# Full 128-token sample tile in the retention, smaller first loads, ones on TensorE at both ends, and the first head's values in a misc PSUM buffer

## The chip, the cores and the metric

The kernel runs on one core of one Trainium2 chip. The metric is the device time of one execution in microseconds (us). The version before takes a median of 1504.3 us over three runs (1504.21 to 1505.61).

## The reference

One step of a hybrid decoder layer over N = 320 tokens: a prompt of 256 and 8 samples of 8 tokens. One input projection feeds two groups of heads: 64 S5 groups (a complex diagonal scan, GELU, a sigmoid GLU) and 8 retention heads. Then an output projection, a SwiGLU feed-forward part and a last RMSNorm.

```python
h = rms_norm(x, norm_mix)
proj = h @ w_in
u, q, k, v, g = jnp.split(proj, [...], axis=-1)
s5_out, s5_re, s5_im = s5_mixer(u, ...)
...
# retention, per head, per chunk of tokens
scores = jnp.einsum('bhnd,bhmd->bhnm', qc, kc) * mask
o = jnp.einsum('bhnm,bhme->bhne', scores, vc) + jnp.einsum('bhnd,bhde->bhne', qc, r) * q_decay
r_new = r * chunk_decay + jnp.einsum('bhmd,bhme->bhde', kc * k_decay, vc)
...
o = (o - mu) * lax.rsqrt(var + NORM_EPS)          # per head
ret_out = jax.nn.silu(g) * o * ret_gn_w
x = x + jnp.concatenate([s5_out, ret_out], axis=-1) @ w_out
h2 = rms_norm(x, norm_ffn)
x = x + (jax.nn.silu(h2 @ w_gate) * (h2 @ w_up)) @ w_ffn_out
y = rms_norm(x, norm_final)
```

D_MODEL is 2048, the head dimension 128, D_FF 5632; all is float32.

## The kernel before

All activations lie transposed: features on the 128 partitions, the 320 tokens along the free axis (0 to 255 the prompt, 256 to 319 the samples). A float32 product is made of three fast ones: each operand is split into `hi` (rounded) and `lo` (the rest), and `gemm` (L122) issues hi·hi, hi·lo and lo·hi for each 128-row tile of the contraction. A weight tile of 512 KB goes through `wload` (L108): SP's DMA to `raw`, ScalarE casts `hi`, VectorE subtracts `lo`. Such a chain runs for each of the 420 weight loads, and TensorE consumes them one after another.

TensorE's order is written by the program itself (`manual_schedule`, L780): instructions stand in the order in which Python issues them. The small work of the retention heads and of the S5 chunks is written as generators. Each yields a delay from the table `DL` (L774), and between two k-tiles of a GEMM `run_due` (L86) runs those that are due by a made-up clock, `clk.now`, which every matmul advances by a cost that the call gives: 0.4 a k-tile in `gemm`, 0.12 a transpose in `tr`, the first argument of `mm`. So a changed cost, or a matmul more or less, can shift where later small work lands between the k-tiles. Orders on VectorE and ScalarE come from a scheduler with priorities (`tc.high_priority`).

PSUM: two accumulators `acc` for GEMMs (L125); two `misc` buffers (L222) that transposes, scores (`pss`), state products (`psr`, `psu`) and the S5's `pk_` and `pt` share; `po` one; `pb` and `py` one each for S5.

The front (L784 to L826) computes the first two S5 inputs from raw x while x streams in: four chunks c of 640 KB of x with two weight pieces of 256 KB each, split by `split_x` (L248). Chunk 0's x comes in two halves. GEMMs go to `py0` and `pb0`. Then come the RMSNorm's sums (`rstd_bcast`, L181, whose reciprocal root `rsqrt`, L170, works on integers and three Newton steps), then q, k, v (`ps_p`) of head 0, each rotated by `rot` (L594). Heads follow: `do_q`, `do_k`, `do_v`, `do_g`, and S5's input `do_u`.

A head, in `head_k` (L609) and `head_v` (L631): transposes of k (`pst`) and v (`pst2`) in pieces of 128, 128 and 64 tokens; `kd`, the decayed k; `pss`, scores; `sm`, `smp`, masked scores; `po`, outputs, in which the samples' part is `smp` times vT plus eight small products of `qg` with the samples' state `rt`; `psr`, the prompt's new state; `pn`, outputs transposed back; then `update` (L698): `psu`, two products of `kd` and `vb`, which VectorE adds to `rt`.

S5's chunk: `bst` and `kst` give `pb` (L531), VectorE multiplies it by `tab` (`t`), forms `ends` and `w`, scans (L551), multiplies again (`v`); ScalarE and VectorE do the GELU of the chunk before (`y`, `u`).

The tail (L1061): last sums of squares (`ps_r`, `ps_l`), reciprocal root on VectorE, `ps_r2` broadcasts it by six passes, and x1 is scaled and stored.

## Time and profile before

| what | us |
|---|---|
| median of three runs | 1504.3 |
| the profiled execution | 1504.93 |
| its span | 1503.0 |
| TensorE busy | 1471.0 |
| VectorE busy | 865.7 |
| ScalarE busy | 607.5 |
| mean granted TensorE clock | 0.992 |

The page's second part cuts the span into 40 slices of 37.6 us and gives the busy tenths of each engine:

```profile
PE   8989999999999999999999999999999999999996
DVE  8987767877655674444444444445444444444454
ACT  5545444544434553333333333333333333333352
PEclk9999999999999999999999999999999999999998
```

The first slice and the last are those with idle TensorE; VectorE is fullest in the first eight slices or so, the heads' part. In the chain of waits:

```profile
PE 68%; DVE 0%; ACT 0%; issue 0%; DVEq 0%
```

The chain that ended last runs along TensorE. In the rows of a timeline the first number is the start in us from the span's start, the second the duration, then engine, line, operation, output and inputs, and in brackets how long the engine was idle before it and what released it.

### The profile page before, as it was taken

The page shows a single profiled execution, that of the slowest core. Times are in us where ns is not written, and L with a number is a line of the kernel's source. Part 1 is how long each engine was busy: PE and PEld are TensorE (multiplying, and loading weights), DVE is VectorE, ACT ScalarE, POOL GpSimd, SP SyncE. Part 2 cuts the span into 40 slices and gives each one's busy share as a digit, 9 for nine tenths or more (in the row PEclk, how much of TensorE's full clock was granted, in tenths as well). Part 3 has the DMA queues.
Part 4 walks back from the last instruction along what each step waited for, and adds up shares of the span by engine and source line. Part 5 has one row for each costly group of instructions (what it writes and reads, how often), then busy time and mean ns, then how long its engine had stood idle before and what let it go on. Part 6 is the DMA issues. An engine that isn't in the chain of part 4 may idle for free.

```text
span 1503.0 us, 26157 instructions
## 1 busy us (share of the span) xinstructions
PE 1471.0 (98%) x10554; PEld 1441.3 (96%) x10554; DVE 865.7 (58%) x1502; ACT 607.5 (40%) x967; POOL 79.6 (5%) x167
## 2 busy tenths in 40 slices
PE   8989999999999999999999999999999999999996
PEld 7989999898999999999999999999999999999996
DVE  8987767877655674444444444445444444444454
ACT  5545444544434553333333333333333333333352
POOL 1331310300000000000000000000000000000001
PEclk9999999999999999999999999999999999999998
DMA  8343444342464444444444445544444544434442
GB/s 284 127 153 119 140 138 147 125 144 94 143 228 142 153 144 166 149 146 155 150 146 154 130 144 158 167 147 153 145 126 151 181 144 153 151 124 150 149 146 108
DMA packets 77335, 224.49 MB, mean 149 GB/s; under 512 B 14752, under 2 KB 26400, under 8 KB 77216
## 3 DMA queue, kind: packets, MB, share of 16 engines
q1 hardware_dynamic: 77216, 222.83, 45.3%
q8 instruction: 83, 1.36, 0.4%
q14 instruction: 36, 0.29, 0.1%
HBM read 213.84 MB, written 7.63 MB: 147 GB/s over the span
## 4 chain that ended last, share of the span: by engine, by line
PE 68%; DVE 0%; ACT 0%; issue 0%; DVEq 0%
PE ps_fg L128 7%; PE ps_fo L128 7%; PE ps_fo L130 7%; PE ps_fu L128 7%; PE ps_fg L130 7%; PE ps_fu L130 7%; PE ps_fu L129 7%; PE ps_fg L129 7%; PE ps_fo L129 7%; PE ps_o L129 1%; PE ps_o L128 1%; PE ps_o L130 1%; PE ps_g L129 1%; PE ps_g L130 1%; PE ps_g L128 1%; DVE x L163 0%
## 5 line engine op out<-in xcount | busy, mean ns | idle before, releaser
L118 DVE TENSOR_TENSOR lo<-raw,hi 128x1024 fp32r<-128x1024 f32 (+1 forms) x420 | 471.4, 1123 | 410.9 <-ACT hi L117 410.6
L117 ACT CAST hi<-raw 128x1024 fp32r<-128x1024 f32 (+1 forms) x420 | 406.4, 968 | 732.4 <-PE ps_fo L129 189.3
L128 PE MATMUL ps_fo<-ahi,hi 128*128 128x320 f32 x704 | 217.5, 309 | 0.0
L129 PE MATMUL ps_fo<-alo,hi 128*128 128x320 f32 x704 | 217.5, 309 | 0.0
L128 PE MATMUL ps_fg<-hhi,hi 128*128 128x320 f32 x704 | 217.5, 309 | 0.0
L130 PE MATMUL ps_fo<-ahi,lo 128*128 128x320 f32 x704 | 217.5, 309 | 0.0
L129 PE MATMUL ps_fg<-hlo,hi 128*128 128x320 f32 x704 | 217.4, 309 | 0.0
L129 PE MATMUL ps_fu<-hlo,hi 128*128 128x320 f32 x704 | 217.4, 309 | 0.0
L128 PE MATMUL ps_fu<-hhi,hi 128*128 128x320 f32 x704 | 217.4, 309 | 0.0
L130 PE MATMUL ps_fg<-hhi,lo 128*128 128x320 f32 x704 | 217.4, 309 | 0.0
L130 PE MATMUL ps_fu<-hhi,lo 128*128 128x320 f32 x704 | 217.4, 309 | 0.0
L128 PE MATMUL ps_p<-xhi,hi 128*128 128x320 f32 x592 | 191.1, 323 | 1.4 <-ACT v__757 L751 1.4
L130 PE MATMUL ps_p<-xhi,lo 128*128 128x320 f32 x592 | 184.4, 311 | 0.0
L129 PE MATMUL ps_p<-xlo,hi 128*128 128x320 f32 x592 | 184.3, 311 | 0.0
L129 PEld LDWEIGHTS ps_fg<-hlo,hi 128*128 128x128 f32 x704 | 132.4, 188 | 0.0
L128 PEld LDWEIGHTS ps_fo<-ahi,hi 128*128 128x128 f32 x704 | 132.4, 188 | 0.0
L128 PEld LDWEIGHTS ps_fu<-hhi,hi 128*128 128x128 f32 x704 | 132.4, 188 | 0.0
L129 PEld LDWEIGHTS ps_fu<-hlo,hi 128*128 128x128 f32 x704 | 132.4, 188 | 0.0
L130 PEld LDWEIGHTS ps_fo<-ahi,lo 128*128 128x128 f32 x704 | 132.4, 188 | 0.0
L128 PEld LDWEIGHTS ps_fg<-hhi,hi 128*128 128x128 f32 x704 | 132.4, 188 | 0.0
L130 PEld LDWEIGHTS ps_fu<-hhi,lo 128*128 128x128 f32 x704 | 132.4, 188 | 0.0
L130 PEld LDWEIGHTS ps_fg<-hhi,lo 128*128 128x128 f32 x704 | 132.3, 188 | 0.0
(402 smaller groups left out, 1978.6 us busy)
## 6 DMA issues: line engine op xcount, KB each, us to landing
raw<-w_fi SPq DMA_DIRECT2D x176, 512.0 KB, 3.6
raw<-w_in SPq DMA_DIRECT2D x76, 512.0 KB, 3.9
raw<-w_fo SPq DMA_DIRECT2D x64, 512.0 KB, 3.5
raw<-w_out SPq DMA_DIRECT2D x32, 512.0 KB, 3.6
raw<-w_fo SPq DMA_DIRECT2D x64, 192.0 KB, 2.4
rt<-r SPq DMA_DIRECT2D x8, 512.0 KB, 4.0
rs_o<-rt SPq DMA_DIRECT2D x8, 512.0 KB, 3.3
raw<-w_glu SPq DMA_DIRECT2D x8, 512.0 KB, 3.6
```

The lines of the kernel that those rows point to most:

```text
L117: act.copy(hi[:, :m], raw[:, :m])
L118: dve.tensor_tensor(lo[:, :m], raw[:, :m], f(hi[:, :m]), SUB)
L128: pe.matmul(ps, hi, xhi[:, k], start=k == 0, stop=False)
L129: pe.matmul(ps, hi, xlo[:, k], start=False, stop=False)
L130: pe.matmul(ps, lo, xhi[:, k], start=False, stop=k == nk - 1)
```

## The change

The edits, by place:

- **Retention's sample tile.** Transposes of k and v now take tokens 192 to 319, so the samples sit in partitions 64 to 127 of a full tile; `smp`, `bmk`, `vb` and the masks move there (mask rows of prompt tokens are zero). The samples' `po` products with `smp` are issued ahead of the eight `qg` products. The cost of one `pss` product rises from 0.11 to 0.22.
- **`rsqrt`**: the shift and the multiply become one operation.
- **Front**: `vec` is loaded by ScalarE's queue; x and the first weights come in pieces of k-tiles (0,2), (2,4), (4,8) and so on, with x's first two tiles one by one; `split_x` puts three of the first four xhi on ScalarE; TensorE's blocks follow the pieces.
- **`keep_warm`**: matmuls on ones into an unread accumulator: 8 ahead of the first GEMM, 3 and 9 in the last norm.
- **Head 0's v** accumulates in a misc buffer (`ps_pv`); `finish_norm` copies `rtok` once.

```diff
         clk.now += 0.12
+    onesr = ones.bitcast(F32R)
+    def keep_warm(n):
+        pt = ps_acc.tile([P, 512], F32, name="warm_ps", tag="acc", bufs=2)
+        for _ in range(n):
+            pe.matmul(pt, onesr, onesr.unsqueeze(1).to_broadcast([P, 4, P]), start=True, stop=True)
...
     def rsqrt(t, y, tmp):
-        ts(tmp.bitcast(I32), t.bitcast(I32), 1, ALU.logical_shift_right)
-        ts(y.bitcast(I32), tmp.bitcast(I32), -1, MUL, 0x9EF759DF, ADD)
+        ts(y.bitcast(I32), t.bitcast(I32), -0.5, MUL, float(0x1EF759DF), ADD)
...
         ps = sums(acc, "ps_r")
+        if last is not None:
+            keep_warm(3)
...
                 stt(ms, sums(last(), "ps_l"), -0.5 / D, ms, MUL, ADD)
+            if last is not None:
+                keep_warm(9)
...
     kdc = mp.tile([P, H, 3], F32, name="kdc")
-    bmk = mp.tile([64, 4], F32, name="bmk")
+    bmk = mp.tile([P, 4], F32, name="bmk")
...
         pool.memset(qgs[i], 0.0)
-    smp = mp.tile([64, NB, 32], F32, name="smp")
+    smp = mp.tile([P, NB, 32], F32, name="smp")
...
             k = 4 * c + i
-            if c == 0 or c == 3 and i % 2:
+            if k == 0 or c == 3 and i % 2:
...
     def head_k(h, q_, qg, k_, R):
...
         pst = misc("pst")
-        for i in range(3):
-            m = P if i < 2 else 64
-            tr(pst[:m, P * i:P * i + P], k_[:, P * i:P * i + m])
+        for i, s in enumerate(STARTS):
+            tr(pst[:, P * i:P * i + P], k_[:, s:s + P])
...
         for i in range(3):
-            m = P if i < 2 else 64
-            act.mul(kd[:m, i], pst[:m, P * i:P * i + P], kdc[:m, h, i:i + 1])
+            act.mul(kd[:, i], pst[:, P * i:P * i + P], kdc[:, h, i:i + 1])
...
         mm(0.22, pss[:, 256:384], k_[:, P:256], q_[:, P:256], start=True, stop=True)
-        mm(0.11, pss[0:64, 384:448], k_[:, 256:320], q_[:, 256:320], start=True, stop=True)
+        mm(0.22, pss[:, 384:448], k_[:, 192:320], q_[:, 256:320], start=True, stop=True)
...
         tt(sm[:, 256:384], pss[:, 256:384], mk[:, 0:P], MUL)
-        tt(smp[:, :, 0:NS], pss[0:64, 384:448].rearrange("p (b t) -> p b t", t=NS),
-           mk[0:64, NP:320].rearrange("p (b t) -> p b t", t=NS), MUL)
+        tt(smp[64:128, :, 0:NS], pss[64:128, 384:448].rearrange("p (b t) -> p b t", t=NS),
+           mk[64:128, NP:320].rearrange("p (b t) -> p b t", t=NS), MUL)
...
     def head_v(h, v_, qg, rt, R):
...
         pst2 = misc("pst2")
-        for i in range(3):
-            m = P if i < 2 else 64
-            tr(pst2[:m, P * i:P * i + P], v_[:, P * i:P * i + m])
+        for i, s in enumerate(STARTS):
+            tr(pst2[:, P * i:P * i + P], v_[:, s:s + P])
...
         for i in range(3):
-            m = P if i < 2 else 64
-            act.mul(vT[:m, i], pst2[:m, P * i:P * i + P], rtok[:m, i:i + 1])
-        vb = mp.tile([64, 4, P], F32, name="vb", tag="vb", bufs=1)
-        pool.tensor_tensor(vb, vT[0:64, 2].unsqueeze(1).to_broadcast([64, 4, P]),
-                           bmk.unsqueeze(2).to_broadcast([64, 4, P]), MUL)
+            act.mul(vT[:, i], pst2[:, P * i:P * i + P], rtok[:, i:i + 1])
+        vb = mp.tile([P, 4, P], F32, name="vb", tag="vb", bufs=1)
+        pool.tensor_tensor(vb[64:128], vT[64:128, 2].unsqueeze(1).to_broadcast([64, 4, P]),
+                           bmk[64:128].unsqueeze(2).to_broadcast([64, 4, P]), MUL)
...
         mm(0.22, po[:, 1], sm[:, 256:384], vT[:, 1], start=False, stop=True)
+        for g in range(2):
+            mm(0.22, po[:, 2 + g], smp[:, 4 * g:4 * g + 4].rearrange("p b t -> p (b t)"), vT[:, 2],
+               start=g == 0, stop=False, skip_group_check=True)
...
             for j in range(4):
-                mm(0.06, po[32 * j:32 * j + 32, 2 + g], qg[:, 4 * g + j], rt[:, 4 * g + j], start=True,
-                   stop=False, tile_position=(0, 32 * j))
-            mm(0.22, po[:, 2 + g], smp[:, 4 * g:4 * g + 4].rearrange("p b t -> p (b t)"), vT[0:64, 2],
-               start=False, stop=True)
+                mm(0.06, po[32 * j:32 * j + 32, 2 + g], qg[:, 4 * g + j], rt[:, 4 * g + j], start=False,
+                   stop=True, tile_position=(0, 32 * j), skip_group_check=True)
...
         for i in range(2):
-            mm(0.43, psu[i], kd[32 * i:32 * i + 32, 2], vb[32 * i:32 * i + 32], start=True, stop=True,
-               tile_position=(32 * i, 0))
+            r = slice(64 + 32 * i, 96 + 32 * i)
+            mm(0.43, psu[i], kd[r, 2], vb[r], start=True, stop=True, tile_position=(64 + 32 * i, 0))
...
         with tc.manual_schedule(engines={mybir.EngineType.SP}):
-            sp.dma_start(vec, vecs)
-            for c in range(4):
-                if c == 0:
-                    sp.dma_start(xrs[0][:, 0:2], xT[:, 0:2])
-                else:
-                    sp.dma_start(xrs[c], xT[:, 4 * c:4 * c + 4])
+            act.dma_start(vec, vecs)
+            k0 = 0
+            for b, k1 in enumerate((2, 4, 8, 12, 16)):
+                c, q = k0 // 4, slice(k0 % 8, (k1 - 1) % 8 + 1)
                 for i in range(2):
-                    if c % 2 == 0:
+                    if k0 % 8 == 0:
...
                                               for n in ("hi", "lo")])
-                    raw, hi, lo = ws[i][-1]
-                    q = slice(4 * (c % 2), 4 * (c % 2) + 4)
-                    sp.dma_start(raw[:, q], w_in[i, :, 4 * c:4 * c + 4])
-                    if c == i == 0:
-                        sp.dma_start(xrs[0][:, 2:4], xT[:, 2:4])
-                if c == 1:
+                xs = [slice(0, 1), slice(1, 2)] if not b else [slice(k0 % 4, (k1 - 1) % 4 + 1)]
+                for i in range(2):
+                    if i < len(xs):
+                        sp.dma_start(xrs[c][:, xs[i]], xT[:, 4 * c + xs[i].start:4 * c + xs[i].stop])
+                    sp.dma_start(ws[i][-1][0][:, q], w_in[i, :, k0:k1])
+                if b == 2:
                     sp.dma_start(prm, s5p)
-                split_x(c, 0, 2 if c == 0 else 4)
...
                     raw, hi, lo = ws[i][-1]
+                    if i < len(xs):
+                        split_x(c, xs[i].start, xs[i].stop)
...
                     last_ins["lo"] = dve.tensor_tensor(lo[:, q], raw[:, q], f(hi[:, q]), SUB)
-                    if c == i == 0:
-                        split_x(0, 2, 4)
+                k0 = k1
...
     ps0, ps1 = py0[:, :N], pb0[:, 0, :N]
-    for k0 in range(0, KT, 4):
+    keep_warm(8)
+    for k0, k1 in ((0, 2), (2, 4), (4, 8), (8, 12), (12, 16)):
         for i, ps in enumerate((ps0, ps1)):
-            for k in range(k0, k0 + 4):
+            for k in range(k0, k1):
...
     def finish_norm():
         next(rg)
-        act.copy(rtok[:, 0:2], ytok[0][:, 0:2])
-        act.copy(rtok[0:64, 2:3], ytok[0][64:128, 2:3])
+        act.copy(rtok, ytok[0])
...
     pq = gemm("ps_p", w_in[8], KT, xhi, xlo, ps=pb0[:, 1, :N])
-    pk, pv = proj(9), proj(10)
+    pk = proj(9)
+    pv = gemm("ps_p", w_in[10], KT, xhi, xlo, ps=misc("ps_pv")[:, :N])
...
     sm = np.where((df >= 0) & same, gam[:, None, None] ** np.maximum(df, 0), 0.0) * sc
-    A["masks"] = c(np.concatenate([mk, np.concatenate([sm, sm], 1)], 2).astype(f))
+    A["masks"] = c(np.concatenate([mk, np.concatenate([np.zeros_like(sm), sm], 1)], 2).astype(f))
...
         kd[:, :, i] = gam[None, :] ** (NP - 1 - (P * i + np.arange(P)[:, None])) * sc
-    kd[:64, :, 2] = gam[None, :] ** (NS - 1 - (tt_[:, None] % 8)) * sc
+    kd[64:, :, 2] = gam[None, :] ** (NS - 1 - (tt_[:, None] % 8)) * sc
     A["kdec"] = kd.astype(f)
-    A["bmask"] = c((tt_[:, None] // 8 % 4 == np.arange(4)[None, :]).astype(f))
+    A["bmask"] = c((np.arange(P)[:, None] // 8 % 4 == np.arange(4)[None, :]).astype(f))
...
```

What the change moves on the engines, by the two programs' orders (operation, output and inputs, shape, and the semaphores that an instruction waits for; a line of "..." stands for rows left out, behind a row of ps_p for k-tiles of the GEMM that runs between, three matmuls each).

TensorE between heads 5 and 6, where head 5's `psu`, S5's `pb` and head 6's `pst` and `pss` lie within one GEMM of `ps_p`. Before:

```order
L97 MATMUL psu<-vb,kd 128x512 [waits PE_49,Activation_49,Pool_49]
L97 MATMUL psu<-vb,kd 128x512 [waits PE_49,Activation_49]
L97 MATMUL pb<-kst,bst 128x80 [waits DMAHW6_49,DMAHW7_49,DMAHW1_49,DMAHW0_49]
...
L97 MATMUL pb<-kst,bst 128x80 x4
L128 MATMUL ps_p<-xhi,hi 128x320
...
L102 MATMUL pst<-ident,k__4124 128x128 [waits DVE_49]
...
L102 MATMUL pst<-ident,k__4124 64x128
L97 MATMUL pss<-q__4022,k__4124 128x256 [waits DVE_49]
...
L97 MATMUL pss<-q__4022,k__4124 64x64
```

And after:

```order
L97 MATMUL pb<-kst,bst 128x80 [waits DMAHW3_49,DMAHW4_49,DMAHW2_49,DMAHW1_49]
...
L97 MATMUL pb<-kst,bst 128x80 x4
L97 MATMUL psu<-vb,kd 128x512 [waits PE_49,Activation_49,Pool_49]
L97 MATMUL psu<-vb,kd 128x512 [waits PE_49,Activation_49]
L136 MATMUL ps_p<-xhi,hi 128x320
...
L102 MATMUL pst<-ident,k__4132 128x128 [waits DVE_49]
L102 MATMUL pst<-ident,k__4132 128x128 x2
L97 MATMUL pss<-q__4030,k__4132 128x256 [waits Activation_49]
L97 MATMUL pss<-q__4030,k__4132 128x128
L97 MATMUL pss<-q__4030,k__4132 128x64
```

`pb` and `psu` have changed places, one k-tile later; `pst` follows after four k-tiles where it followed `pb` after three; and `pss`, which waited for VectorE, now waits for ScalarE.

VectorE at the same place, head 6's k being rotated (`k_`, `sw`), S5's chunk (`t` to `w`) and head 5's state (`rt`). Before:

```order
L163 TENSOR_TENSOR sw<-sw,csr 128x320
L163 TENSOR_TENSOR k__4124<-k__4124,sw 128x320 [waits DVE_49]
L167 SCALAR_TENSOR_TENSOR rt<-rt,psu 128x512 [waits PE_49] x2
L163 TENSOR_TENSOR t_4172<-pb,tab 128x512 [waits PE_49,Pool_49]
L163 TENSOR_TENSOR t_4173<-pb,tab 128x512 [waits Pool_49]
```

And after:

```order
L171 TENSOR_TENSOR t_4170<-pb,tab 128x512 [waits PE_49,Pool_49]
L171 TENSOR_TENSOR k__4132<-k__4132,sw 128x320 [waits DVE_49]
L171 TENSOR_TENSOR y_4007<-y_4007,y_4006 128x320 [waits DMAHW3_49,DMAHW5_49,DMAHW2_49,DMAHW7_49,DMAHW1_49,Activation_49]
L171 TENSOR_TENSOR t_4171<-pb,tab 128x512 [waits Pool_49]
L175 SCALAR_TENSOR_TENSOR u_111<-y_4007,y_4006 128x320 [waits Activation_49]
L171 TENSOR_TENSOR ends<-pb,lx_123 128x32
L171 TENSOR_TENSOR w<-t_4170,t_4171 128x256 [waits DVE_49]
L171 TENSOR_TENSOR w<-t_4170,t_4171 128x256
L171 TENSOR_TENSOR ends<-pb,lx_123 128x32 [waits Activation_49]
L563 SCALAR_TENSOR_TENSOR w<-d_126,w 128x512 [waits DVE_49]
L175 SCALAR_TENSOR_TENSOR rt<-rt,psu 128x512 [waits PE_49]
```

`rt`, which came ahead of the chunk's work, now comes behind its scan (L563).

VectorE between heads 6 and 7, the same names one head on. Before:

```order
L163 TENSOR_TENSOR ends<-pb,lx_123 128x32
L163 TENSOR_TENSOR w<-t_4641,t_4642 128x256 [waits DVE_49]
L163 TENSOR_TENSOR w<-t_4641,t_4642 128x256
L167 SCALAR_TENSOR_TENSOR u_111<-y_4505,y_4504 128x320 [waits Activation_49]
L163 TENSOR_TENSOR ends<-pb,lx_123 128x32 [waits Activation_49]
L551 SCALAR_TENSOR_TENSOR w<-d_127,w 128x512 [waits DVE_49]
L167 SCALAR_TENSOR_TENSOR rt<-rt,psu 128x512 [waits PE_49]
```

And after:

```order
L171 TENSOR_TENSOR ends<-pb,lx_123 128x32
L171 TENSOR_TENSOR w<-t_4645,t_4646 128x256 [waits DVE_49]
L171 TENSOR_TENSOR w<-t_4645,t_4646 128x256
L175 SCALAR_TENSOR_TENSOR rt<-rt,psu 128x512 [waits PE_49]
L126 TENSOR_TENSOR lo<-raw,hi 128x1024 [waits DMAHW1_49,Activation_49]
```

`rt` has moved ahead of `u` and the scan. On TensorE `psu` there stands four k-tiles behind `pb`, where it stood one behind; on both sides the first `rt` frees the buffer that the second `psu` takes.

## The prediction

> **What bounds the kernel now.** I read the page's busy shares first, then TensorE's waits, then windows of the stretches where it waits.
>
> ```profile
> PE 1471.0 (98%) x10554; PEld 1441.3 (96%) x10554; DVE 865.7 (58%) x1502; ACT 607.5 (40%) x967; POOL 79.6 (5%) x167
> PE py L823 <- ACT hi L810: 7.3, 1, 7.3
> PE psu L97 <- DVE rt L167: 3.2, 1, 3.2
> PE ps_r L97 <- DVE ry L167: 2.5, 1, 2.5
> PE pk__1151 L97 <- DVE rt L167: 2.4, 1, 2.4
> PE pt L102 <- DVE retp L167: 1.6, 1, 1.6
> PE ps_p L128 <- ACT v__757 L751: 1.4, 1, 1.4
> PEld py L825 <- DVE lo L811: 0.5, 3, 0.2
> ```
>
> The page's first row says that TensorE works for 98% of the span; the waits (engine, tile, releaser: total, times, longest) name the rest. 7.3 us go at the start, 1.4 + 1.6 + 2.4 in the first 90 us, 3.2 later in the heads, 2.5 at the end. No edit touches the feed-forward part, where it never waits. So the change is worth what it does to these waits, to new ones, and to the granted clock behind each.
>
> ```profile
> 20.00:86.00 66.00, 60.80 (x420) 57.45 (x418) 64.91 (x222) 35.27 (x71) 24.96 (x54) 1.00 0.48 156
> 86.00:90.00 4.00, 3.63 (x27) 3.22 (x28) 0.91 (x2) 2.04 (x8) 0.87 (x4) 0.57 0.74 261
> ```
>
> In these windows (length, busy PE, PEld, DVE, ACT, POOL, then granted clock) VectorE is busy for 64.9 of the 66 us from 20 to 86. It, not TensorE, sets the end of that stretch. And the 2.4 us wait before pk_ is followed by a clock of 0.57 for four us, a stretch at half speed: 4 x 0.43 = 1.7 us lost.
>
> **The front: -0.5 us.**
>
> ```profile
> 0.73 0.38 SPq L787 DMA_DIRECT2D vec<-vecs  x1
> 4.33 1.73 DVE L157 TENSOR_SCALAR xhi<-u,vec 128x320 fp32r<-128x320 f32 x2 [4.33 <-DMA u<-xT]
> 7.23 0.69 DVE L811 TENSOR_TENSOR lo<-raw,hi 128x512 fp32r<-128x512 f32 x1 [0.25 <-ACT hi L810]
> 9.79 1.93 ACT L255 ACTIVATE xhi<-u,vec 128x320 fp32r<-128x320 f32 x4 [1.00 <-DMA u<-xT]
> 7.25 0.64 PE L823 MATMUL py<-xhi,hi 128*128 128x320 f32 x1 [7.25 <-ACT hi L810]
> 10.54 0.47 PE L825 MATMUL py<-xhi,lo 128*128 128x320 f32 x1
> 10.81 0.47 PE L823 MATMUL pb<-xhi,hi 128*128 128x320 f32 x1
> 13.03 1.93 ACT L255 ACTIVATE xhi<-retp,vec 128x320 fp32r<-128x320 f32 x4 [0.28 <-DMA retp<-xT]
> 12.00:20.00 8.00, 8.00 (x55) 7.68 (x54) 7.93 (x20) 7.72 (x14) 0.00 (x0) 1.00 1.03 406
> ```
>
> The first matmul starts at 7.25, when the first 256 KB of weights have landed and been split. Halved loads and `vec` on ScalarE's queue let it start some 2 to 2.5 us sooner (an estimate: half the bytes of x and weights ahead of it, and one issue of SP less). The eight matmuls on ones take 8 x 0.27 x 512/320 = 3.4 us at the start's slow clock (0.27 from 10.54 to 10.81 for 320 columns) and fit before it. But the second piece of x, 640 KB, lands at 9.79 only after the same bytes as before, and the third at 13.03: ScalarE waits for DMA at both, and the DMA share is 1.03 from 12 to 20. `vec` leaving SP's queue puts all loads one issue, some 0.4 us, earlier; shorter rows take part of that back. From the second piece on TensorE already waits three times for VectorE's lo parts (0.5 us in all). What it gains ahead of them it waits away there. I take -0.3 us for the loads.
>
> The first head's v accumulator in a misc buffer removes the 1.4 us wait of ps_p for v_, but TensorE then meets VectorE's next results sooner: k_, retp and rt are all VectorE's, and it is full until 86 us. VectorE itself saves one operation in the norm and one in head 0 (0.2 us each by the tail's row below). So the waits at 78 and 86 us shrink by its gain, not by TensorE's: -0.5 us in all, with the half clock behind pk_ kept. Bounds: +1.2 (a further half-clock window, 1.7) and -2.2 (that stretch gone).
>
> **The 128-row tile: +0.3 us.**
>
> ```profile
> L102 PEld LDWEIGHTS pst<-ident,k__4124 128*128 128x128 f32 x2 | 0.3, 138 | 0.0
> L102 PEld LDWEIGHTS pst<-ident,k__4124 128*64 128x64 f32 x1 | 0.1, 111 | 0.0
> ```
>
> The third transpose of k_ and of v_ now loads 128 columns: 138 for 111 ns (the number before the last bar), for each of 2 x 8, 0.43 us at most. The third product of pss grows alike, 8 times. Against it stand two accumulating products and eight small ones that stay as many as before. I take +0.3, bounds 0 and +0.7.
>
> **A new wait behind head 5: +5.5 us.** By the order, pb is now issued ahead of psu, and the next head's transposes (pst) four k-tiles behind psu. pst needs a misc buffer, both of which psu holds until VectorE has added rt. VectorE now does rt behind the scan.
>
> ```profile
> 328.22 2.01 PE L97 MATMUL pb<-kst,bst 128*128 128x80 f32 x16
> 330.03 0.39 PE L128 MATMUL ps_p<-xhi,hi 128*128 128x320 f32 x1
> 330.55 0.31 PE L128 MATMUL ps_p<-xhi,hi 128*128 128x320 f32 x1
> 330.99 0.31 PE L128 MATMUL ps_p<-xhi,hi 128*128 128x320 f32 x1
> 328.52 1.28 DVE L167 SCALAR_TENSOR_TENSOR rt<-rt,psu 128x512 f32<-128x512 f32 x2
> 330.34 1.29 DVE L163 TENSOR_TENSOR t<-pb,tab 128x512 f32<-128x512 f32 x2 [0.54 <-PE pb L97]
> 331.55 0.48 DVE L163 TENSOR_TENSOR y<-y,y 128x320 f32<-128x320 f32 x1
> 331.94 0.18 DVE L163 TENSOR_TENSOR ends<-pb,lx 128x32 f32<-128x32 f32 x1
> 332.05 0.75 DVE L163 TENSOR_TENSOR w<-t,t 128x256 f32<-128x256 f32 x2
> 333.85 0.48 DVE L167 SCALAR_TENSOR_TENSOR u<-y,y 128x320 f32<-128x320 f32 x1
> 334.35 1.21 DVE L551 TENSOR_TENSOR_SCAN w<-d,w 128x512 f32<-128x512 f32 x1
> 332.99 0.86 ACT L618 ACTIVATE kd<-pst,kdc 128x128 f32<-128x128 f32 x3
> 327.16 1.13 PE L97 MATMUL psu<-vb,kd 32*128 32x512 f32 x4
> ```
>
> Before (start, duration), rt came first, 328.52 to 329.8, and pst found a free buffer. Now count from the end of pb (330.03 here, the next instruction's start). TensorE reaches pst after psu (328.22 - 327.16 = 1.1 us) and four k-tiles of three matmuls (4 x 0.44, from 330.55 to 330.99): 2.8 us. VectorE begins t 0.3 us after pb, and does by start-to-start steps t (0.6), the last step of k_ (0.4), y (0.4), t (0.6), u (0.4), ends (0.1), w (0.7), ends (0.1), scan (1.1), rt (0.6): 5.4 us. TensorE waits 2.6 us, 2.7 with the hand-over. pss behind it takes the buffer that pst fills and waits for kd, 0.86 us and a hand-over, 1.1. That is 3.8 us with two matmul groups stuck behind, the projection and so everything else. ScalarE's tanh between y and u can lengthen it. Nothing covers it: TensorE is in order.
>
> The clock: 2.4 us of waiting before pk_ cost one half-speed stretch, 1.7 us. This wait is longer and broken only by three transposes, so I add 1.7: +5.5. Bounds: 0 (rt earlier than I think) and +7.2 (two stretches, as in the next part).
>
> The Trainium skill, page "TensorE: Matmul & The Clock Gate", section "HAM oscillation — how this bites in real kernels", asks for an idle gap of over about 3.4 us before the clock falls. By it neither part of this wait would cost clock, and the sum would be 1.7 better. The trace disagrees already: the clock fell behind 2.4 us.
>
> **The wait behind head 6: -5.7 us.**
>
> ```profile
> 372.37 1.52 PE L97 MATMUL psu<-vb,kd 32*128 32x512 f32 x2 [3.23 <-DVE rt L167]
> 372.00:380.00 8.00, 7.63 (x26) 6.47 (x27) 4.22 (x8) 2.24 (x5) 0.00 (x0) 0.57 0.30 95
> ```
>
> The second psu waits 3.23 us for the first rt, which stands behind u and the scan. The clock of 0.57 behind it loses 8 x 0.43 = 3.4 us, twice the stretch above: 6.7 in all. Now rt stands right behind w, and psu four k-tiles behind pb. From pb's end: first psu done at 4 x 0.44 + 0.53 = 2.3; VectorE through t, y, ends, w at 0.3 + 1.2 + 0.4 + 0.1 + 0.7 = 2.7, rt at 3.3. Wait: 1.0 us, too short for the clock (1.4 and 1.6 above left it at 1.00). So 6.7 - 1.0 = 5.7 saved; bounds 0 and 6.7.
>
> **The tail: -0.9 us.**
>
> ```profile
> 1490.73 1.62 PE L97 MATMUL ps_r<-ident,ry 128*128 128x128 f32 x6 [2.52 <-DVE ry L167]
> 1490.00:1492.00 2.00, 1.27 (x6) 1.30 (x6) 0.48 (x3) 0.00 (x0) 0.00 (x0) 0.50 0.00 0
> 1488.44 0.17 DVE L157 TENSOR_SCALAR rt<-ms 128x3 int32<-128x3 int32 x1
> 1488.65 0.17 DVE L159 TENSOR_SCALAR ry<-rt 128x3 int32<-128x3 int32 x1
> ```
>
> The reciprocal root loses one of its steps, 0.2 us. Twelve matmuls on ones keep TensorE busy through the wait; the six passes of ps_r at clock 0.50 took 1.62, at full clock half: -0.8. Three of them stand ahead of ps_l and may hold it up by 0.1. Bounds: -1.0 and +0.2 (clock lost all the same, ones in the way).
>
> **Sum.** -0.5 + 0.3 + 5.5 - 5.7 - 0.9 = **-1.3 us**. All this is against the profiled execution: span 1503.0 and 1.9 around it, 1504.93, which lies 0.6 above the median of the runs, 1504.3. Against the median: **1503.0**. A measurement of this kernel can tell about 0.2%, 3.0 us, so this is no change.
>
> **Rivals.**
>
> 1. The shorter front runs through. Starting at about 5 instead of 7.25, and at full clock instead of 0.27 us a matmul up to 11 us (2 us lost), TensorE would gain 2.3 + 2 = 4.3 instead of 0.5: -5.1, 1499.2. The Trainium skill's same page, section "Why this matters for your kernels", has TensorE reach the full clock by some 4 us of continuous work, which the ones give; the trace agrees in the length (slow from 7.25 to 11.1). The start-up wait of 7.3 speaks for it, the lo waits and VectorE's full windows against it. 0.13.
> 2. The wait behind head 5 hardly comes (rt earlier, or a third buffer free), 0 to 1 us: -6.8 to -5.8, about 1498. For it: my count hangs on ten steps. 0.18.
> 3. The wait comes, but the clock holds: -3.0, 1501.3. 0.14.
> 4. Slower: the scan's place. If VectorE comes so late that rt holds psu up behind head 6 as now (gain 0) while the new wait costs two stretches (3.8 + 3.4), the sum is -0.5 + 0.3 + 7.2 - 0.9 = +6.1, 1510.4. It decides from the point where the two places together cost 4.3 us more than forecast (from -1.3 to +3.0). For it: u and scan wait for ScalarE. Against: rt moved ahead of both there. 0.10.
> 5. The ones don't do what they say: the clock at the end falls anyway and the tail gives 0.2 for 0.9. -0.6, 1503.7. 0.11.
>
> **How the numbers follow.** Forecast 0.34. Faster by over 0.2%: rivals 1 and 2 and half of 3, 0.38. Within 0.2%: the forecast, 5, half of 3, 0.52. Slower: 0.10. The range, 1497.5 to 1506.2, takes in rivals 1, 2 and 3 and, upwards, a new wait with two stretches (+1.7) and the front's worse bound (+1.7); the forecast's own is 1500 to 1506.
>
> **What would show it.** In the profile after: first matmul near 5 us, yet chunk two of x landing at 9.4 to 9.8, and py waiting there; no wait of ps_p at 46 us, but pk_ still waiting for rt near 86; a wait of pst for rt near 331 of some 2.7 us with pss behind kd, and the clock low after it; psu behind head 6 waiting 1 us at clock 1.00; ps_r's six passes in some 0.8 us. No pst wait, or the end of VectorE's full stretch 2 us or more earlier than 86, would prove me wrong.

## The result, and the profile after

The change makes the kernel slower. Its median is 1512.87 us over four runs (1510.83 to 1514.6), against 1504.51 over four runs of the kernel before (1504.21 to 1505.61): ratio 1.0054, 95% interval 1.0036 to 1.0071. That lies above the predicted range. The profiled execution took 1513.66 with a span of 1510.0, against 1504.93 and 1503.0: of its 8.7 us more, 7.0 are in the trace. The other 1.7 lie outside the span (3.7 against 1.9), in this one execution; in the three other runs it was 1.9, and in the kernels below 1.8 to 2.6.

First the busy shares of the page after, and TensorE's waits (engine, tile, releaser: total, times, longest):

```profile
PE 1478.7 (98%) x10574; PEld 1450.5 (96%) x10574; DVE 864.6 (57%) x1490; ACT 608.9 (40%) x971; POOL 80.3 (5%) x167
```

```profile
PE pst L102 <- DVE rt L175: 2.5, 1, 2.5
PE pn L102 <- ACT on L679: 2.5, 2, 2.0
PE pk__1164 L97 <- DVE rt L175: 2.4, 1, 2.4
PE py L832 <- ACT hi L819: 2.3, 1, 2.3
PE psu L97 <- DVE retp L175: 2.2, 1, 2.2
PE pt L102 <- DVE retp L175: 1.7, 1, 1.7
PE pst L102 <- DVE cl L171: 1.4, 1, 1.4
...
PE psu L97 <- DVE rt L175: 0.8, 1, 0.8
```

VectorE and ScalarE have as much to do as before. TensorE has 7.7 us more of busy time, but its 20 more instructions, the matmuls on ones, are busy for 7.1 us (3.78 + 0.96 + 2.33) by themselves: the busy shares do not show where the time went. The waits the prediction named are here: pst for rt 2.5 (forecast 2.7), pss for kd 1.0 (1.1), psu for rt 0.8 (1.0), and at the front py, without a forecast of its length, 2.3. Two it did not name stand beside them: psu for retp 2.2, and pn for `on` 2.5, which was 0.5 before. A third, pst for cl 1.4, takes the place of the 1.4 us of ps_p.

Windows after (length, busy PE, PEld, DVE, ACT, POOL, then granted clock, DMA share, GB/s):

```profile
6.00:8.00 2.00, 1.67 (x9) 1.36 (x9) 1.64 (x4) 1.76 (x6) 0.00 (x0) 1.00 0.91 277
10.00:12.00 2.00, 0.38 (x3) 0.11 (x1) 1.19 (x3) 1.78 (x4) 0.00 (x0) 1.00 0.96 326
12.00:17.00 5.00, 3.96 (x16) 3.54 (x17) 4.69 (x13) 3.76 (x9) 0.00 (x0) 0.66 1.03 407
183.00:191.00 8.00, 7.11 (x23) 5.63 (x24) 5.57 (x13) 1.00 (x1) 0.00 (x0) 0.57 0.46 146
281.00:290.00 9.00, 7.01 (x28) 6.30 (x28) 4.25 (x7) 4.61 (x12) 0.00 (x0) 0.62 0.41 117
339.00:348.00 9.00, 6.02 (x23) 5.44 (x24) 8.54 (x17) 2.38 (x9) 0.00 (x0) 0.62 0.38 126
384.00:388.00 4.00, 4.00 (x17) 3.75 (x17) 4.00 (x9) 1.28 (x6) 0.00 (x0) 0.62 0.52 193
```

Behind the waits of psu, pn, pst, py and the last psu, at these places, the clock is low for a stretch. 8 x (1 - 0.57) = 3.4 us are lost behind psu's, 9 x 0.38 = 3.4 each behind pn's and pst's, 5 x 0.34 = 1.7 behind py's and 4 x 0.38 = 1.5 behind the last psu, whose slow stretch runs on to 388.4.

Where the difference arises is seen by comparing when the same projection matmul (counted from the first) starts in two traces. The table gives this lag against the kernel before in us, at places named by the time of the kernel before; the other rows are experiments below. "End" is the last such matmul. Each row comes from one profiled execution. A slow stretch of the clock adds 1.7 or 3.4 us to a lag, and the last section shows that one and the same wait brings such a stretch in one kernel and not in another; so steps of that size are not exact to a microsecond or two.

| kernel | 21 | 126 | 179 | 211 | 267 | 297 | 361 | end |
|---|---|---|---|---|---|---|---|---|
| after | 1.6 | 0.6 | -0.2 | 4.8 | 3.5 | 7.5 | 12.2 | 7.9 |
| after, made-up cost 0.11 | 0.8 | 1.4 | 0.6 | 0.5 | -0.8 | 2.8 | 1.5 | 0.5 |
| before, made-up cost 0.22 | 0.6 | -1.2 | -1.2 | 2.4 | 2.4 | 5.0 | 10.0 | 6.4 |
| before + 128-row tile | 0.5 | -1.4 | -2.1 | -2.3 | -3.5 | -1.6 | -2.9 | -4.0 |
| the same, cost 0.22 | 0.4 | -1.4 | -2.2 | 2.7 | 1.5 | 5.5 | 9.3 | 3.4 |
| best version | 0.0 | -2.3 | -3.0 | -3.2 | -4.4 | -4.1 | -5.4 | -11.7 |

After loses at four places (the front, 179 to 211, 267 to 297, 297 to 361), gains back at one (361 to 396) and a little at each head.

### The profile page after: what moved, and what is told of

It reads as the page before. It is cut to its first block, busy times and chain, and to the rows that moved or that the text cites. A ratio compares the mean times of both kernels' runs of the same rounds, so it can differ in the third digit from the quotient of the medians.

```text
span 1510.0 us, 26190 instructions
## 1 busy us (share of the span) xinstructions
PE 1478.7 (98%) x10574; PEld 1450.5 (96%) x10574; DVE 864.6 (57%) x1490; ACT 608.9 (40%) x971; POOL 80.3 (5%) x167
## 4 chain that ended last, share of the span: by engine, by line
PE 67%; DVE 0%; ACT 0%; DVEq 0%; issue 0%
PE ps_fg L136 7%; PE ps_fo L136 7%; PE ps_fo L137 7%; PE ps_fu L137 7%; PE ps_fg L137 7%; PE ps_fu L136 7%; PE ps_fg L138 7%; PE ps_fu L138 7%; PE ps_fo L138 7%; PE ps_o L137 1%; PE ps_o L138 1%; PE ps_o L136 1%; PE ps_g L137 1%; PE ps_g L138 1%; PE ps_g L136 1%; DVE x L171 0%
## 5 line engine op out<-in xcount | busy, mean ns | idle before, releaser
L136 PE MATMUL ps_p<-xhi,hi 128*128 128x320 f32 x576 | 187.8, 326 | 0.0
L138 PE MATMUL ps_p<-xhi,lo 128*128 128x320 f32 x576 | 181.1, 314 | 0.0
```

The source lines that it names most:

```text
L136: pe.matmul(ps, hi, xhi[:, k], start=k == 0, stop=False)
L138: pe.matmul(ps, lo, xhi[:, k], start=False, stop=k == nk - 1)
```

## The experiments

All ratios are against the kernel before, run beside each kernel on the same chip; n is the number of runs.

### The made-up cost alone

It is the one number that the instructions themselves never see: it only moves `clk.now`, and with it which k-tile the later small work follows.

```diff
-        mm(0.22, pss[:, 384:448], k_[:, 192:320], q_[:, 256:320], start=True, stop=True)
+        mm(0.11, pss[:, 384:448], k_[:, 192:320], q_[:, 256:320], start=True, stop=True)
```

> The changed kernel with one number put back: the made-up cost of the samples' scores product is 0.11 again (the product itself stays 128 rows). Theory 'the planner's order': the cost alone moved the heads' small work between the k-tiles, and with it the waits near 181 (psu), 280 (pn) and 338 us (pst) with their half clock. They go, the wait of psu near 368 with its two half-speed stretches returns: some -11.5 + 4.7, so about 1505 (1502.5 to 1506). Theory 'the 128-row tile itself' (longer weight loads and transposes, samples in the upper partitions): the time stays at 1511 to 1514.

The reverse in the kernel before:

```diff
-        mm(0.11, pss[0:64, 384:448], k_[:, 256:320], q_[:, 256:320], start=True, stop=True)
+        mm(0.22, pss[0:64, 384:448], k_[:, 256:320], q_[:, 256:320], start=True, stop=True)
```

> The kernel before with that one number changed from 0.11 to 0.22 and nothing else; all instructions are the same, only where the small work stands differs. Theory 'the planner's order': about 1511 (1509 to 1514), with waits of psu near 181, pn near 280 and pst near 338 us. Theory 'the 128-row tile itself': 1504.5, no change.

After with 0.11: 1504.22 (n 11), ratio 0.9995 [0.9987, 1.0004]. Before with 0.22: 1511.64 (n 5), ratio 1.0048 [1.0035, 1.006]. The cost is worth 7.0 us in the kernel before and 8.7 in after, as much as the whole change loses (8.4). In TensorE's order it moves the products psu in three heads of eight: by three k-tiles later in head 2 (behind 873 projection matmuls instead of 864), one earlier in head 5 (1548 for 1551; not "one k-tile later", as "The change" has it), two later in head 6 (1728 for 1722). The prediction had costed the last two.

The first, in the timelines of TensorE and VectorE (start, duration); before:

```profile
179.53 2.27 PE L97 MATMUL psu<-vb,kd 32*128 32x512 f32 x4
180.28 0.28 DVE L167 SCALAR_TENSOR_TENSOR retp<-pn,vec,sg 128x64 f32<-128x64 f32 x1
182.87 0.48 DVE L163 TENSOR_TENSOR q__2313<-ps_p,csr 128x320 f32<-128x320 f32 x1
```

and after:

```profile
180.61 1.12 PE L97 MATMUL psu<-vb,kd 32*128 32x512 f32 x2
183.89 1.19 PE L97 MATMUL psu<-vb,kd 32*128 32x512 f32 x1 [2.16 <-DVE retp L175]
180.07 0.48 DVE L175 SCALAR_TENSOR_TENSOR retp<-pn,vec,sg 128x256 f32<-128x256 f32 x1
181.93 0.48 DVE L171 TENSOR_TENSOR q__2324<-ps_p,csr 128x320 f32<-128x320 f32 x1
183.06 0.49 DVE L171 TENSOR_TENSOR q__2324<-q__2324,sw 128x320 f32<-128x320 f32 x1
183.47 0.28 DVE L175 SCALAR_TENSOR_TENSOR retp<-pn,vec,sg 128x64 f32<-128x64 f32 x1
```

The second psu needs the buffer that pn holds until VectorE has formed both pieces of retp. Before, psu stood where a projection ends; now three k-tiles of the next one come first, so the projection q has ended and VectorE rotates q between the two pieces of retp. TensorE waits 2.16 us, then runs a stretch at half speed that costs 3.4: +5.0 from 179 to 211 in the table's row of after, and +5.0 between the two kernels with the tile (0.0 to 5.0). In the kernel before with cost 0.22 the same wait costs +3.6, with a shorter stretch (1.7) behind it.

### VectorE's place for rt

```diff
+        with tc.high_priority(offset=300):
             for i in range(2):
                 ...
                 stt(rv, rv, float(GAM[h] ** NS), psu[i].rearrange("p (b e) -> p b e", e=P), MUL, ADD)
```

> The changed kernel, in which VectorE's two rt operations of each head get a higher priority, so that they stand close behind psu instead of behind the scan. TensorE's order is that of the changed kernel. Theory 'the waits come from VectorE's place for what frees the misc buffers': the wait of pst near 338 us (2.5, with pss 1.0 behind it and two half-speed stretches) goes, that of psu behind head 6 shrinks below 0.5; the waits near 181 (retp) and 280 us (on) stay. 5.5 to 7 us less than the changed kernel: 1505 to 1507. Rival 'something else, the kd or the scan itself, holds TensorE there': 1511 to 1513.

After, without this edit, the head behind 335 reads (TensorE, then VectorE):

```profile
341.01 0.90 PE L102 MATMUL pst<-ident,k__4132 128*128 128x128 f32 x3 [2.52 <-DVE rt L175]
342.88 1.97 PE L97 MATMUL pss<-q__4030,k__4132 128*128 128x256 f32 x6 [0.97 <-ACT kd L628]
339.16 1.22 DVE L563 TENSOR_TENSOR_SCAN w<-d,w 128x512 f32<-128x512 f32 x1
340.29 0.66 DVE L175 SCALAR_TENSOR_TENSOR rt<-rt,psu 128x512 f32<-128x512 f32 x1
```

With it:

```profile
337.90 0.49 PE L102 MATMUL pst<-ident,k__4132 128*128 128x128 f32 x3
338.23 0.99 PE L97 MATMUL pss<-q__4030,k__4132 128*128 128x256 f32 x6
336.17 0.68 DVE L175 SCALAR_TENSOR_TENSOR rt<-rt,psu 128x512 f32<-128x512 f32 x1
341.33 1.22 DVE L563 TENSOR_TENSOR_SCAN w<-d,w 128x512 f32<-128x512 f32 x1
```

rt now comes ahead of the scan, and neither pst nor pss waits. The median falls to 1505.05 (n 11), ratio 0.9999 [0.999, 1.0008]: 7.8 us less than after. The wait behind head 5 is what the prediction said it is; the one in head 2 stays, as 1.7 us on rt instead of 2.2 on retp, with the clock low behind it as long as in after.

### The 128-row tile alone

The tile's edits of `head_k`, `head_v` and `update`, with the masks and the copy of `rtok` that belong to them, with cost 0.11, and the same with 0.22:

> The kernel before with the 128-row sample tile alone, made-up cost 0.11, so that TensorE's order outside po is that of before. Theory 'fewer changes of tile shape': TensorE's po and psr block takes 2.25 instead of 2.77 us and pss 0.80 instead of 1.01 in each of the 8 heads, 5.8 us in all; where no later wait takes it back: 1498 to 1501. Rival (the prediction's term): +0.3, 1504 to 1505.

> The same with the made-up cost 0.22, TensorE's order then that of the changed kernel. Theory 'the order takes the tile's gain back': waits of psu near 181, pn near 280, pst near 338 us with half-speed stretches; 7 to 9 us above the tile alone, 1506 to 1509. Rival: the tile's gain shortens these waits, 1504 or less.

1499.9 (n 11, one of them an outlier at 5085 us that no other run resembles), ratio 0.9975 [0.9966, 0.9984]; and 1509.07 (n 5), ratio 1.0039 [1.0027, 1.0051]. So the tile gains 4.3 us, and the cost takes 9.2. TensorE's output block of one head before:

```profile
58.81 0.83 PE L97 MATMUL po<-vT,sm 128*128 128x128 f32 x6
59.57 0.43 PE L97 MATMUL po<-rt,qg 128*32 128x128 f32 x8
59.92 0.49 PE L97 MATMUL po<-vT,smp 64*128 64x128 f32 x2
60.34 0.43 PE L97 MATMUL po<-rt,qg 128*32 128x128 f32 x8
60.69 0.49 PE L97 MATMUL po<-vT,smp 64*128 64x128 f32 x2
61.11 0.71 PE L97 MATMUL psr<-vT,kd 128*128 128x128 f32 x4
61.58 0.40 PE L128 MATMUL ps_p<-xhi,hi 128*128 128x320 f32 x1
```

and after:

```profile
60.02 0.83 PE L97 MATMUL po<-vT,sm 128*128 128x128 f32 x6
60.68 0.61 PE L97 MATMUL po<-vT,smp 128*128 128x128 f32 x4
61.22 0.64 PE L97 MATMUL po<-rt,qg 128*32 128x128 f32 x16
61.80 0.71 PE L97 MATMUL psr<-vT,kd 128*128 128x128 f32 x4
62.27 0.39 PE L136 MATMUL ps_p<-xhi,hi 128*128 128x320 f32 x1
```

The same number of products, but from the first to the next projection 2.77 us before (61.58 - 58.81) and 2.25 after. Each smp product costs 0.21 before (0.42 for two) and 0.14 after (0.54 for four). The scores' block loses another 0.2, and the lag of the tile's row falls by about 0.7 at most heads (-1.4 at 126, -2.1 at 179). Only from 267 to 297 it rises, by 1.9: in that execution the clock is low for a stretch at 276, behind a wait of 1.0 us for retp that the kernel before has too, at full clock.

### The front

The loads and blocks of the change with the eight matmuls on ones; without them; and with nine more of them in the gap ahead of the second chunk:

```diff
+    keep_warm(8)
+    for k0, k1 in ((0, 2), (2, 4), (4, 8), (8, 12), (12, 16)):
+        if k0 == 4:
+            keep_warm(9)
```

> The kernel before with the changed loads and the eight matmuls on ones at the start, all else as before. Theory 'the front is bound by the second piece of x': first matmul near 4.7 us, TensorE waits some 2 us for that piece near 10 us and the clock falls behind it, the time ends within 1504.0 to 1506.0. Rival 'the shorter front runs through': 1500 to 1502.

> The kernel before with the changed loads and no ones at the start. Theory 'ones bring the full clock too early, so that it falls again while TensorE waits for x': without them the first matmuls run at half speed while nothing is late, and the time is 1504 to 1505.5. Rival 'the wait near 10 us costs the clock either way': as with the ones, 1506 to 1507.

> The kernel before with the changed loads and eight ones, and nine more ones where TensorE waits some 2.4 us for the second piece of x. Theory 'what the front loses is the half-speed stretch behind that wait': the stretch goes, 1.7 us less than without the nine, 1504.3 to 1505.3, no gain over before since x's second piece lands when it did. Rival 'the loss is in the loads or VectorE': 1506 or more.

1506.53, 1506.91 and 1506.41 (n 11 each), ratios 1.0011 [1.0002, 1.002], 1.0013 [1.0004, 1.0022] and 1.001 [1.0001, 1.0019]. All three lose 1.6 to 2.1 us, with ones and without, so the ones are not the cause; the nine more gained 0.1 us, not the 1.7 expected. What is left are the loads, with the splits and the order of blocks that go with them. (In these three the first matmul starts at 5.92, where after has 4.71: VectorE's first split takes 2.30 us there and 0.42 in after. Why is not known.) ScalarE's splits of x's second and third pieces, after:

```profile
10.22 1.92 ACT L267 ACTIVATE xhi<-u,vec 128x320 fp32r<-128x320 f32 x4 [1.95 <-DMA u<-xT]
14.51 1.92 ACT L267 ACTIVATE xhi<-retp,vec 128x320 fp32r<-128x320 f32 x4 [1.17 <-DMA retp<-xT]
```

They started at 9.79 and 13.03 before: the first matmul starts 2.5 us sooner (4.71), but x's third piece is split 1.5 us later. Both splits waited for the DMA. The windows of before, beside those of after above:

```profile
6.00:8.00 2.00, 0.75 (x3) 0.53 (x3) 1.75 (x5) 0.62 (x1) 0.00 (x0) 1.00 1.03 396
10.00:12.00 2.00, 2.00 (x12) 2.00 (x12) 1.65 (x5) 2.00 (x5) 0.00 (x0) 1.00 1.03 404
```

396 and 404 GB/s before, 277 and 326 after, with DMA less than fully busy (0.91 and 0.96 for 1.03). Other windows differ less or the other way (8 to 10 us: 324 before, 340 after), but the sum holds in every trace: by 12 us the six kernels with the changed loads had moved 2.90 to 3.05 MB, and the eleven with pieces of the old size 3.06 to 3.29; the third piece was split at 14.3 to 14.6 in the six, at 13.0 to 14.2 in the eleven.

Is it the number of issues in SP's queue, or the short pieces? In the kernel before, two small loads more were issued ahead of x's second piece; in another, four short weight pieces went to ScalarE's queue:

```diff
+                if c == 0:
+                    sp.dma_start(kdc, kdec)
+                    sp.dma_start(bmk, bmask)
```

> The kernel before, with two tiny loads that come later anyway (kdc, bmk; 12 KB and 1 KB) issued by SP ahead of x's second piece: as many issues of SP ahead of it as in the changed front, but the rows of x and weights as long as before. All orders on the other engines stay. Theory 'the issues': x's second piece is issued near 4.0 instead of 3.1 us, its third piece reaches ScalarE near 14.5 instead of 13.0 to 13.7, and the time is 1506 to 1507. Rival 'the short rows': third piece at 13.8 or sooner, time 1504 to 1505.3.

```diff
-                    sp.dma_start(ws[i][-1][0][:, q], w_in[i, :, k0:k1])
+                    (act if b < 2 else sp).dma_start(ws[i][-1][0][:, q], w_in[i, :, k0:k1])
```

> The kernel before with the changed loads and no ones, but the four small weight pieces issued by ScalarE's queue behind vec instead of SP's. Theory 'SP's issues hold back the second and third piece of x': x's second piece is issued near 2.1 instead of 4.0 us and lands 0.5 us or more earlier, the third some 1 us earlier; the time falls from 1506.9 to 1504 to 1505.5. Rival 'the short rows themselves are slow': 1506 or more.

Two more issues cost nothing: 1504.97 (n 11), ratio 1.0 [0.9991, 1.0009], x's third piece split at 13.38. The other, 1514.23 (n 5), ratio 1.0058 [1.0046, 1.0071], tells nothing of the loads by its time: ScalarE's own work came late, VectorE's order shifted, and new waits stand between 30 and 90 us, where it falls 9 us behind. But its trace has the same short pieces, at 397 GB/s from 6 to 8 us and 3.25 MB by 12. So neither two more issues nor the short pieces by themselves are shown to be the cause; which part of the changed loads slows them stays open.

### Smaller parts

The reciprocal root's shorter form alone, in the kernel before:

```diff
-        ts(tmp.bitcast(I32), t.bitcast(I32), 1, ALU.logical_shift_right)
-        ts(y.bitcast(I32), tmp.bitcast(I32), -1, MUL, 0x9EF759DF, ADD)
+        ts(y.bitcast(I32), t.bitcast(I32), -0.5, MUL, float(0x1EF759DF), ADD)
```

> The kernel before with the reciprocal root one operation shorter, nothing else; TensorE's order stays that of before. Theory 'a shorter chain moves ScalarE's queue': head 4's four on operations are now queued with a weight cast and the two sw copies among them, TensorE waits for on near 277 us some 2 us, and a half-speed stretch follows: 1506 to 1508. Rival 'one operation less': 0.2 to 0.6 us less than before, about 1504.2.

An operation less, and slower: 1506.44 (n 11), ratio 1.0015 [1.0006, 1.0024]. Its trace shows ScalarE splitting the group of four `on` of head 4, which was one of 1.50 us at 275.78 before:

```profile
275.56 0.46 ACT L668 ACTIVATE on<-po,gy 128x128 f32<-128x128 f32 x1 [8.21 <-DVE gy L167]
275.92 1.04 ACT L117 CAST hi<-raw 128x1024 fp32r<-128x1024 f32 x1
276.98 0.42 ACT L600 COPY sw<-ps_p 64x320 f32<-64x320 f32 x1
277.41 0.42 ACT L601 COPY sw<-ps_p 64x320 f32<-64x320 f32 x1
277.86 1.15 ACT L668 ACTIVATE on<-po,gy 128x128 f32<-128x128 f32 x3
```

A cast and two copies slip between, and pn waits (2.1 us in all, 0.5 before). After has the same with two `on` ahead of the cast and two behind it: pn waits 1.96 us:

```profile
282.57 0.82 PE L102 MATMUL pn<-ident,on 128*128 128x128 f32 x2 [1.96 <-ACT on L679]
```

It is the scheduler's order that changed, not the work. In this kernel the clock held behind the split, which cost 1.7 us; the shorter root saved its 0.2 at the very end. The cost of 0.22 alone makes such a split too (before with 0.22: +2.6 from 267 to 297).

Head 0's v in a misc buffer, and the ones at the end:

```diff
-    pk, pv = proj(9), proj(10)
+    pk = proj(9)
+    pv = gemm("ps_p", w_in[10], KT, xhi, xlo, ps=misc("ps_pv")[:, :N])
```

> The kernel before with the first head's v accumulating in a misc buffer, nothing else; TensorE's order stays. Theory 'the wait moves': the 1.4 us of ps_p near 46 us go, a wait of pst for k of some 1.2 us comes near 54: 1504.0 to 1505. Rival 'the wait goes': 1503.2 or less.

```diff
+        if last is not None:
+            keep_warm(3)
...
+            if last is not None:
+                keep_warm(9)
```

> The kernel before with only the three and nine matmuls on ones in the last norm. Theory: the clock holds, the six passes of ps_r take 0.8 instead of 1.6 us: 0.6 to 0.9 us less, 1503.6 to 1503.9. Rival 'the ones stand in the way': 1504.5 or more.

v: 1504.58 (n 11), ratio 1.0001 [0.9993, 1.001]. The wait of 1.4 us at 46 is gone, and pst waits 1.4 for `cl` instead. The tail: 1503.57 (n 11), ratio 0.9991 [0.9983, 1.0], that is -1.1 us, an interval that just reaches no change; in its trace the stretch from the feed-forward part's last matmul to the end is 0.7 shorter than before. In after the six passes ps_r take 0.91 us, where they took 1.62 at half clock before.

### Towards a better version

The tail with rt's priority in the kernel before; that with `vec` on ScalarE's queue as well; and the 128-row tile (cost 0.11), the tail's ones and rt's priority together, all else as before:

> The kernel before with the ones at the end and that same priority for rt. TensorE's order is that of before. Theory: the wait of psu behind head 6 falls from 3.2 to about 1.2 us and the two half-speed stretches behind it go: 3.4 + 2.0 = 5.4 less than the kernel with the ones alone (1503.6): about 1498 (1497 to 1500). Rival 'a wait moves elsewhere': 1501 or more.

> The kernel before with the ones at the end, the priority for rt, and vec loaded by ScalarE's queue (all other loads as before, each issued by SP one place earlier). Theory: all loads land some 0.3 to 0.45 us earlier and VectorE's first stretch with them: 1499.7 to 1500.1 against 1500.3 without. Rival 'the start is bound elsewhere': 1500.3 or more.

> The changed kernel with everything but the 128-row sample tile and the ones at the end taken back (loads, first head's v, reciprocal root, made-up cost 0.11), and with the priority for rt. It differs from the kernel before with ones at the end and that priority (1500.3) only in the tile. Theory 'the tile itself costs next to nothing': 1500.0 to 1501.3. Rival 'the tile costs over 0.1 us a head': 1501.5 or more.

1500.28 (n 5), ratio 0.9965 [0.9952, 0.9977]; 1500.96 (n 8), ratio 0.9969 [0.9958, 0.9979]; 1496.3 (n 5, 1492.58 to 1497.09), ratio 0.9946 [0.9933, 0.996]. The first lies just above its range: in its trace psu's wait behind head 6 has fallen from 3.2 to 0.8, but the clock was low behind it for as long as before. `vec`'s queue changes nothing. The third's expectation still took the tile to cost nothing; it is worth 4.0 here (1496.3 against 1500.28). This kernel, the best version of the lag table, beats both others: 7.7 us below before and some 16 below after. Nearly all of it is the change's own two good parts plus one VectorE priority: -4.3 (tile), -1.1 (tail) and -3.3 (1500.28 against the tail's 1503.57) make -8.7, and 7.7 were measured.

## Why the prediction was wrong

By its own terms, in us; measured values are steps of the lag table in the row of after, or medians where a part ran alone.

| term | predicted | measured |
|---|---|---|
| front | -0.5 | about +2 (after less the tile's row, at 179; loads alone +2.1 in median) |
| 128-row tile | +0.3 | -4.3 (alone) |
| wait behind head 5 | +5.5 | +5.0 (before with cost 0.22) to +6.0 (after less the tile's row) |
| wait behind head 6 | -5.7 | -3.2 (after less the tile's row) to -3.6 (before with cost 0.22) |
| tail | -0.9 | -0.9 |
| wait in head 2 | not in the sum | +5.0 |
| wait in head 4 | not in the sum | +4.0 (+2.1 less the tile's row) |

**The step that failed most** was to cost the shift of TensorE's order at two places. The order shows three heads with a moved psu; the prediction worked through heads 5 and 6, and passed head 2 over, where psu moved by three k-tiles past a projection's end. That cost 5.0. Head 4's 4.0 is not in TensorE's order at all: it comes from ScalarE's, where a shorter reciprocal root and the cost each shift a scheduler's choice, and the prediction costed the shorter root at 0.2 us saved. The two signs that it had named as proof against itself, no wait of pst or an early end of VectorE's full stretch, did not appear; they lay at places that it had costed.

**The tile** had the wrong sign. The prediction priced longer weight loads, which lie beside the matmuls, and said of the products that they "stay as many as before". They do, but each takes less time.

**The front** had the wrong sign. "Halved loads" was worked out in bytes ahead of the first matmul, where it held (4.71 forecast "near 5"), and the rest taken as landing "only after the same bytes as before"; the bytes came more slowly. The step "What it gains ahead of them it waits away there" was right in its kind and too small: TensorE waits 2.33 us for the second chunk, the clock falls at once (0.66 from 12 to 17), and it then runs 1.6 late. That VectorE sets the end of the stretch to 86 us fits the runs: with the loads alone it is as full as before (64.8 of the 66 us). But the prediction took VectorE's own time as given. Its operations from 20 to 86 come 1.4 to 1.7 us later there than in the kernel before, and TensorE with them: 1.6 late at 62 and 2.1 at the end.

**Head 5** was right in place, mechanism and size. In the lag table the stretch from 297 to 361 gives after 4.7, 6.0 without the 1.3 that the tile's row gains there, and the kernel before with cost 0.22 alone 5.0; rt came right behind the scan; pst waited 2.52 and pss 0.97. The waits themselves were 0.3 shorter than forecast (3.5 for 3.8; the forecast's ten steps, with the 0.3 ahead of them, add up to 5.3, not 5.4), and the clock lost 3.4 where 1.7 was taken; in the kernel before with cost 0.22 it lost 1.7.

**Head 6** had the right mechanism and a size too large: psu waits 0.78, but the clock fell for a window all the same (0.62 from 384 to 388). From 361 to the end after gains 4.3, 3.2 without the 1.1 of the tile's row, and the kernel before with cost 0.22 alone 3.6. "Too short for the clock" failed here; in the profiled execution of the best version, with the same wait of 0.8, the clock held, and it gained 6.3 there, 5.2 beside the tile. That execution is the fastest of five (1492.58); the other four took 3.5 to 4.5 us more, at a granted clock of 0.994 to 0.995 for 0.996. So 5.7 was possible, and whether it came could not be read from the wait's length.

**The tail** and **v's wait** came as forecast: the lag falls from 7.9 at the end of the projections to 7.0 at the end of the span, about 0.7 by the ones and 0.2 by the root, and the wait of 1.4 us only moves.

The range failed with the same step: each of its ends was built from the places that were costed. The slower rival's 1510.4 comes near the result, but by a mechanism that did not occur: rt was to hold psu up behind head 6 as before, and it holds it for 0.78 us.

## What to carry to other kernels

A made-up cost, or one operation more or less, that reorders work costs or gains at each place where a row moves: list all of them on all engines (TensorE's, but also VectorE's and ScalarE's orders) before pricing any, and compare two traces by the lag of the same matmul. When a change mixes real work with a shift of order, separate the two: here the tile's real work gained 4 us and the order took 9. An order's waits are cheap to mend once they are seen, as one priority for the release of a PSUM buffer showed.

## What the runs showed of the hardware

- **The same wait cost the clock nothing, one slow stretch or two.** The losses were 1.7 or 3.4 us each (in one trace 5.1), stretches of 3.4 or 6.8 us at half speed. Fourteen of the kernels have a wait of pk_ of 2.3 to 2.4 us near 87 us. Around it the clock held in three of them (1.00 from 84 to 96 us), fell for one stretch in six and for two in five (0.72 there). Seven have the psu wait of 0.78 us behind head 6: the clock held in two, fell once in four, in after among them, and twice in one. The earlier wait of 3.23 us at that place cost two stretches or more in all eleven kernels that have it. So the length of a wait alone does not decide, and a forecast can only give chances. The Trainium skill, page "TensorE: Matmul & The Clock Gate", section "What's actually happening", gives the window in which TensorE's activity is watched as 3413 ns and free-running, not starting with the work. The runs agree with the length, and a window that runs free of the work would explain why equal waits cost differently; no run here shows it by itself. The Trainium skill's same page, section "HAM oscillation — how this bites in real kernels", asks for an idle gap of over about 3.4 us. None of these waits was that long, so by the measurements it is no safe bound.
- **Products of one shape took less time than mixed ones.** The 64-row products between products of 32 columns took 0.21 us each, the 128-row ones behind others of their shape 0.14. Which of the two, the rows or the neighbour, makes the difference was not tried apart.
- **With the front's smaller first loads all loads came more slowly**: 277 GB/s for 396 from 6 to 8 us, 2.90 to 3.05 MB by 12 us for 3.06 to 3.29. The same pieces issued from two queues did not (397 GB/s, 3.25 MB), so the size of the pieces alone is not shown to be the cause.
